# Prompt attention and convolution of a hybrid decoder step: other places in the interleaved order, compressed scores on column quarters, the convolution in five pieces

## The chip, the cores and the metric

The kernel runs on one core of one Trainium2 chip, in float32 throughout. The metric is the device time of one execution in microseconds (us). The engines are TensorE (PE, with PEld for its weight loads), VectorE (DVE), ScalarE (ACT), GpSimd (POOL) and SyncE (SP); SP issues most DMAs and POOL some. Each engine works through its own instructions in the order in which the program gives them to it.

## The reference, cut to what matters

One step of a hybrid decoder layer for 256 prompt rows and 8 sequences of 8 sample rows (320 columns together): a feed-forward half-step, one combined projection, a Mamba-2 mixer (convolution, chunked scan, gate), native sparse attention, a merge, and a second feed-forward half-step. The change touches the convolution and the prompt's attention:

```python
def causal_conv(xbc, conv_state, w, b):
    L = xbc.shape[1]
    xp = jnp.concatenate([conv_state.astype(xbc.dtype), xbc], axis=1)
    y = b + sum(xp[:, k:k + L] * w[k] for k in range(D_CONV))
    return jax.nn.silu(y), xp[:, L:]
...
    s_c = jnp.einsum('bthgd,bnhd->bthgn', q, kc) + bias_qk(dist_c, bias_tab)
    p_c = masked_softmax(s_c, (dist_c >= 0)[None, :, None, None, :])
    o_c = jnp.einsum('bthgn,bnhd->bthgd', p_c, vc)
    # and the same over selected blocks and over a window of the raw keys
    return gates[..., 0:1] * o_c + gates[..., 1:2] * o_s + gates[..., 2:3] * o_w
```

`kc` and `vc` are compressed keys and values, one per 32 rows, so the 256 prompt rows have 8 of them.

## The kernel before, in words

All weight matrices stream once through the core. `dense` (L329 to L355) multiplies one 128x1024 weight tile with the 320 activation columns: the tile comes by DMA, ACT makes its high part (L317, 1 us), DVE its low part (L326, 1.2 us), and PE runs 24 matmuls (8 steps k, three matmuls each, L345 to L347) into a PSUM bank `pd`. I call this a unit. Units follow each other through the whole program and keep PE busy.

Everything else is written as Python generators and put between the matmuls of the units when the program is built. After each k of a unit `dense` calls `S.tick()`. A tick moves a deferred function half a unit of `defer` nearer (`S.defer(2, f)` runs `f` four ticks later, and a unit has eight ticks), and adds half of `RATE[i]` to a credit; for each whole credit one step of a generator is emitted, up to its next `yield`. So RATE 1.5 puts six steps into a unit. Two chains of generators take turns; `pace(i)` sets the rate when a chain comes to a new part. Part 3 is prompt attention, part 4 the scan (`ssd`), part 5 the attention of the samples (`sample_attn`), part 6 `merge_prep`. The order on every engine is thus fixed when the program is built, and an instruction that has to wait holds up all that stands behind it on its engine.

The stretch in question has 24 units of the projection, whose outputs are the channels of the convolution. Behind each, `conv_unit` (L1218) works up its 320 columns:

- at once: POOL copies the old state (`scv`) into `pr`, ACT copies the unit's output into `pr` (L1222, L1223), POOL saves the new state (`ncv`, two small copies) and computes the first tap (`cvo`, L1229);
- four ticks later (`taps`): DVE adds three taps (L1233, three instructions), and directly behind them ACT takes the tanh (L1234);
- eight ticks later (`gate`): DVE forms the output `xbc` (L1237, L1240).

Beside it `prompt_attn` runs over 4 blocks `qc` of 64 queries and 8 pairs of heads `u`, 32 iterations `i`. For each block:

- `build(qc)`: POOL scales the queries into a tile of zeros, `qbp` (L1269, tile `blob`);
- `cmp_a(qc)`: PE multiplies the queries with the 2, 4, 6 or 8 compressed keys (L1276, tile `ps_pt`), then ten small instructions on DVE and ACT make a softmax of it;
- `cmp_b(qc, q)`, q = 0 and 1: PE transposes four heads' weights (L1298), ACT copies them out (L1299).

For each iteration: `scores` (PE L1305 into a bank `sc`, DVE bias and minimum L1311, ACT exponentials L1314), `norm` (DVE reciprocal L1322, POOL scaling L1325), `transposes` (PE L1337 into a bank `pt`, ACT copy L1338) and `values` (PE L1354 into the one bank `po`, which ACT empties at the end of a block, L1358). `scores` runs four iterations ahead of `values`. Behind `values` the block in work prepares the next: `build` at u = 1, `cmp_a` at u = 2, both `cmp_b` at u = 4.

The second chain first turns the values of the prompt into rows (`values_tok`, PE L1023 and L1029, ACT copies), then handles the samples' new keys (`new_keys`, PE L1041, L1055, L1068) and compressed keys (`cmp_sample`, PE L1127, L1182, L1200), which uses much DVE.

PSUM has eight banks: three `pd`, two `sc`, two `pt`, one `po`. A bank can be written again when its last reader is through.

## Time and profile before

| What | Value |
|---|---|
| Runs shown | 1339.16, 1340.64, 1348.0 us, median 1340.64 |
| Profiled execution | 1347.1 us, span from first to last instruction 1345.5 us |
| PE busy | 1277.8 us, 95% of the span |
| DVE busy | 877.8 us, 65% |
| ACT busy | 591.8 us, 44% |
| POOL busy | 371.0 us, 28% |
| Granted TensorE clock, mean | 0.973 |

PE does nearly all the time, so a place can be worth something only where PE stands still or where its clock is below full. A digit in the profile's slices hides the place of such a stand; the waits by engine, the sums by stretch and the timeline show it. A wait in these views is the idle time of an engine directly before an instruction, with the instruction elsewhere that ended it.

### The profile page before, as it was taken

The page shows a single profiled execution, that of the slowest core. Times are in us where ns is not written, and L with a number is a line of the kernel's source. Part 1 is how long each engine was busy: PE and PEld are TensorE (multiplying, and loading weights), DVE is VectorE, ACT ScalarE, POOL GpSimd, SP SyncE. Part 2 cuts the span into 40 slices and gives each one's busy share as a digit, 9 for nine tenths or more (in the row PEclk, how much of TensorE's full clock was granted, in tenths as well). Part 3 has the DMA queues.
Part 4 walks back from the last instruction along what each step waited for, and adds up shares of the span by engine and source line. Part 5 has one row for each costly group of instructions (what it writes and reads, how often), then busy time and mean ns, then how long its engine had stood idle before and what let it go on. Part 6 is the DMA issues. An engine that isn't in the chain of part 4 may idle for free. (4 is left out here: it accounts for less than half of the span.)

```text
span 1345.5 us, 28237 instructions
## 1 busy us (share of the span) xinstructions
PE 1277.8 (95%) x10609; PEld 1158.7 (86%) x10609; DVE 877.8 (65%) x1872; ACT 591.8 (44%) x1154; POOL 371.0 (28%) x624
## 2 busy tenths in 40 slices
PE   7999999999999998889999798998989999999998
PEld 7799999999989897777797576776758999999998
DVE  5267766755565767886568688778657766666543
ACT  4254444445435323455654243456554444333331
POOL 2123221322200225765435553344430010000000
PEclk8699999999989998999999999999999999999999
DMA  8256665766654435531157676899982544444553
GB/s 270 97 161 222 215 215 169 222 220 217 199 181 138 141 136 190 187 113 64 48 180 245 196 239 197 295 351 326 342 292 92 177 134 143 156 156 145 156 165 91
DMA packets 98467, 251.65 MB, mean 187 GB/s; under 512 B 14632, under 2 KB 41273, under 8 KB 96377
## 3 DMA queue, kind: packets, MB, share of 16 engines
q1 hardware_dynamic: 81370, 198.24, 44.9%
q0 software_dynamic: 16960, 51.61, 11.2%
q8 instruction: 84, 1.38, 0.4%
q14 instruction: 53, 0.43, 0.1%
HBM read 235.07 MB, written 23.10 MB: 192 GB/s over the span
## 5 line engine op out<-in xcount | busy, mean ns | idle before, releaser
L345 PE MATMUL ps_pd<-hh,wh 128*128 128x320 f32 x1320 | 444.5, 337 | 5.7 <-ACT hh L261 1.8
L326 DVE TENSOR_TENSOR wl<-wraw,wh 128x1024 fp32r<-128x1024 f32 (+1 forms) x245 | 305.4, 1248 | 183.2 <-ACT wh L317 176.2
L347 PE MATMUL ps_pd<-hh,wl 128*128 128x320 f32 x1320 | 416.4, 315 | 1.5 <-DVE wl L326 1.5
L346 PE MATMUL ps_pd<-hl,wh 128*128 128x320 f32 x1320 | 416.8, 316 | 0.6 <-DVE hl L454 0.3
L317 ACT CAST wh<-wraw 128x1024 fp32r<-128x1024 f32 (+1 forms) x245 | 252.2, 1032 | 139.7 <-PE ps_pd L346 102.2
L345 PEld LDWEIGHTS ps_pd<-hh,wh 128*128 128x128 f32 x1320 | 255.1, 193 | 30.1 <-issue 16.2
L346 PEld LDWEIGHTS ps_pd<-hl,wh 128*128 128x128 f32 x1320 | 255.7, 194 | 9.2 <-issue 4.8
L347 PEld LDWEIGHTS ps_pd<-hh,wl 128*128 128x128 f32 x1320 | 255.2, 193 | 2.2 <-DVE wl L326 2.2
L345 PE MATMUL ps_pd<-ah,wh 128*128 128x320 f32 x352 | 109.5, 311 | 0.0
L347 PE MATMUL ps_pd<-ah,wl 128*128 128x320 f32 x352 | 108.9, 309 | 0.0
L580 DVE TENSOR_TENSOR pgl<-pg,pgh 128x512 fp32r<-128x512 f32 x128 | 82.5, 685 | 30.0 <-ACT pgh L573 29.9
L346 PE MATMUL ps_pd<-al,wh 128*128 128x320 f32 x320 | 98.8, 309 | 0.0
L568 POOL DMA_DIRECT2D pg<-in_cache x136 | 74.2, 546 | 76.8 <-DVE pgl L580 30.8
L238 POOL TENSOR_SCALAR ah<-ff 128x320 fp32r<-128x320 f32 x44 | 20.0, 454 | 268.7 <-DVE ff L482 268.7
L477 ACT ACTIVATE sg<-sg 128x320 f32<-128x320 f32 x44 | 20.8, 472 | 134.2 <-DVE sg L476 134.1
L573 ACT CAST pgh<-pg 128x512 fp32r<-128x512 f32 x128 | 72.6, 616 | 9.1 <-PE ps_sc L702 8.8
L1419 POOL DMA_DIRECT2D KV<-in_cache x102 | 54.9, 539 | 76.7 <-PE ps_po L1506 43.2
L701 PE MATMUL ps_sc<-pgh,w1h 128*128 128x256 f32 x256 | 68.1, 287 | 0.8 <-ACT pgh L573 0.8
L702 PE MATMUL ps_sc<-pgh,w1l 128*128 128x256 f32 x256 | 68.1, 288 | 0.0
L345 PEld LDWEIGHTS ps_pd<-ah,wh 128*128 128x128 f32 x352 | 66.2, 188 | 0.5
L347 PEld LDWEIGHTS ps_pd<-ah,wl 128*128 128x128 f32 x352 | 66.1, 188 | 0.0
L346 PEld LDWEIGHTS ps_pd<-al,wh 128*128 128x128 f32 x320 | 60.2, 188 | 0.0
(474 smaller groups left out, 2219.6 us busy)
## 6 DMA issues: line engine op xcount, KB each, us to landing
wraw<-in_wproj SPq DMA_DIRECT2D x77, 512.0 KB
KV<-in_cache POOLq DMA_DIRECT2D x102, 256.0 KB, 5.6
wraw<-in_w1in SPq DMA_DIRECT2D x44, 512.0 KB
wraw<-in_w2in SPq DMA_DIRECT2D x44, 512.0 KB
pg<-in_cache POOLq DMA_DIRECT2D x136, 128.0 KB, 4.1
pg<-in_cache SPq DMA_DIRECT2D x120, 128.0 KB
wraw<-in_w1out SPq DMA_DIRECT2D x16, 512.0 KB
h<-in_ssm SPq DMA_DIRECT2D x32, 256.0 KB
```

The lines of the kernel that those rows point to most:

```text
L317: a.copy(h[:, :n], st["raw"][i][:, :n])
L326: v.tensor_tensor(l[:, :n], st["raw"].pop(i)[:, :n], st["hl"][i][0][:, :n], op=ALU.subtract)
L345: pe.matmul(out, wh[:, s], xh[:, kk, :], start=kk == 0, stop=False)
L346: pe.matmul(out, wh[:, s], xl[:, kk, :], start=False, stop=False)
L347: pe.matmul(out, wl[:, s], xh[:, kk, :], start=False, stop=kk == K - 1)
L477: a.activation(s, s, AF.Silu)
L568: e.dma_start(page(s, half)[:, i, :], I["cache"][ds(r, 1), :, 256 * c : 256 * c + 256].rearrange("o p f -> p (o f)"))
L573: a.copy(h[:, 8 * half : 8 * half + 8, :], page(s, half)[:, :, 64 * q : 64 * q + 64])
L580: v.tensor_tensor(l[:, 8 * half : 8 * half + 8, :], page(s, half)[:, :, 64 * q : 64 * q + 64], h[:, 8 * half : 8 * half + 8, :], op=ALU.su ...
L701: pe.matmul(ph, wh[:, j, :], h[:, :, j, :], start=q + j == 0, stop=False)
L702: pe.matmul(ph, wl[:, j, :], h[:, :, j, :], start=False, stop=False)
L1419: e.dma_start(t[:, j, :], I["cache"][ds(r, 1), :, 512:1024].rearrange("o p f -> p (o f)"))
```

## The change: what it does

Eight things, in the order of the diff:

1. `RATE[3]` (prompt attention) 1.5 to 1.55, `RATE[4]` (scan) 0.88 to 0.9.
2. The second transpose of `values_tok` uses a bank `sc` instead of `pt`.
3. `cmp_sample` has its four waiting steps spread between its reductions, and one step more before `mb`.
4. The convolution has five pieces: copies at once, then the first tap with the `ncv` copies (2 ticks), three taps (5 ticks), tanh (8 ticks), gate (11 ticks).
5. `cmp_a` runs each pair of heads as four matmuls of 32 query columns, each into its own quarter of the PSUM partitions, instead of one of 128 columns.
6. The first block: `build(0)`, five empty steps, then `scores(0)`, `cmp_a(0)`, `scores(1)` to `scores(3)`, `cmp_b(0, 0)`, `transposes(0)`, `cmp_b(0, 1)`, with steps between.
7. The next blocks: `build` at u = 0, `cmp_a` at u = 3.
8. The two `cmp_b` come at u = 5 and u = 6 instead of together at u = 4.

```diff
-RATE = (0.59, 1.2, 0.9, 1.5, 0.88, 0.57, 1.0)
+RATE = (0.59, 1.2, 0.9, 1.55, 0.9, 0.57, 1.0)
...
         for t in range(2):
-            pv = bank("pt")
+            pv = bank("sc" if t else "pt")
...
         for j in range(2):
             v.reduce_sum(rk[:, j, :], U[j], axis=AX.X)
+            yield
             v.reduce_sum(cs[:, j, :], U[j].rearrange("p i j -> p j i"), axis=AX.X)
-            yield from wait(2)
+            yield
...
         mb = pq.tile([128, 4, 2, 32], F32, name="mb")
+        yield
...
-        gcopy(ncv[:, i, 0:3], pr[:, 256:259])
-        gcopy(ncv[:, i, 3:27].rearrange("p (b k) -> p b k", b=NB), ps_[:, :, 8:11])
...
-        g.tensor_scalar(o, pr[:, 0:344], w(0), cwh[:, 96 + i : 97 + i], op0=ALU.mult, op1=ALU.add)
+
+        def first():
+            g.tensor_scalar(o, pr[:, 0:344], w(0), cwh[:, 96 + i : 97 + i], op0=ALU.mult, op1=ALU.add)
+            gcopy(ncv[:, i, 0:3], pr[:, 256:259])
+            gcopy(ncv[:, i, 3:27].rearrange("p (b k) -> p b k", b=NB), ps_[:, :, 8:11])
 
         def taps():
             for k in range(1, 4):
                 v.scalar_tensor_tensor(o, pr[:, k : k + 344], w(k), o, op0=ALU.mult, op1=ALU.add)
+
+        def tanh():
             a.activation(th, o, AF.Tanh)
...
-        S.defer(2, taps)
-        S.defer(4, gate)
+        S.defer(1, first)
+        S.defer(2.5, taps)
+        S.defer(4, tanh)
+        S.defer(5.5, gate)
...
             for u in range(8):
-                pe.matmul(pc[:, u, :nb], qbp[qc % 2][:, u, :], kTp[:, u // 4, :nb], start=True, stop=True)
+                for c in range(4):
+                    o = slice(32 * c, 32 * c + 32)
+                    pe.matmul(pc[o, u, :nb], qbp[qc % 2][:, u, o], kTp[:, u // 4, :nb], start=True, stop=True)
...
         build(0)
-        yield from wait(2)
+        yield from wait(5)
+        scores(0)
+        yield
         cmp_a(0)
-        yield from wait(4)
+        yield
+        scores(1)
+        yield
+        norm(0)
+        scores(2)
+        yield
+        norm(1)
+        scores(3)
+        yield
+        norm(2)
         cmp_b(0, 0)
+        yield
+        transposes(0)
+        yield
         cmp_b(0, 1)
-        for i in range(4):
-            scores(i)
-            yield
-            if i:
-                norm(i - 1)
-        transposes(0)
         yield
...
-                if u == 1:
+                if u == 0:
                     build(qc + 1)
-                elif u == 2:
+                elif u == 3:
                     cmp_a(qc + 1)
-                elif u == 4:
-                    cmp_b(qc + 1, 0)
-                    cmp_b(qc + 1, 1)
+                elif u in (5, 6):
+                    cmp_b(qc + 1, u - 5)
```

How the order changes is seen best on three engines. The first place is ACT at the end of block 0, where `po` is emptied (the copy `qn<-ps_po`). `cvt` is the tanh of the convolution, `pr` its input, `wh` the high part of a weight tile, `pT` and `blob` are transposes of `transposes` and `cmp_b`, `pS` the exponentials. Before:

```order
L1234 ACTIVATE cvt<-cvo 128x344
L1338 COPY pT<-ps_pt 128x256
L1314 ACTIVATE pS,pm<-pS,pm 128x128 x2
L1222 COPY pr_4873<-ps_pd 128x256
L1223 COPY pr_4873<-ps_pd 128x8x8
L317 CAST wh<-wraw 128x1024
L1358 COPY qn<-ps_po 128x8x64
```

With the change, on the same engine at the same place:

```order
L1240 ACTIVATE cvt<-cvo 128x344
L1309 COPY blob<-ps_pt 4x512
L1224 COPY pr_4873<-ps_pd 128x256
L1225 COPY pr_4873<-ps_pd 128x8x8
L317 CAST wh<-wraw 128x1024
L1348 COPY pT<-ps_pt 128x256
L1324 ACTIVATE pS,pm<-pS,pm 128x128 x2
L1368 COPY qn<-ps_po 128x8x64
L1240 ACTIVATE cvt<-cvo 128x344
```

The tanh that stood in the middle of a unit now stands at its end, directly before the copies of the next unit's output, three ticks behind its taps; what ACT does between two tanhs is the same as before in another order, and one copy of `cmp_b` comes into it. The emptying of `po` stands directly before a tanh in both.

The second place is POOL around `build(1)` (`blob<-qn`), with the scaling of `norm` (`pS<-pS,pm,gtp`) and the convolution's pieces. Before:

```order
L1308 MEMSET pS 128x2x64
L238 TENSOR_SCALAR pr_4873<-scv 128x8x3
L238 TENSOR_SCALAR ncv<-pr_4873 128x3
L238 TENSOR_SCALAR ncv<-pr_4873 128x24
L1229 TENSOR_SCALAR cvo<-pr_4873,cwh 128x344
L1269 TENSOR_SCALAR blob<-qn 64x8x64 x2
L1325 TENSOR_SCALAR pS<-pS,pm,gtp 128x64 x2
```

With the change, on POOL around the same `build(1)`:

```order
L1318 MEMSET pS 128x2x64
L238 TENSOR_SCALAR pr_4873<-scv 128x8x3
L1277 TENSOR_SCALAR blob<-qn 64x8x64 x2
L1231 TENSOR_SCALAR cvo<-pr_4873,cwh 128x344
L238 TENSOR_SCALAR ncv<-pr_4873 128x3
L238 TENSOR_SCALAR ncv<-pr_4873 128x24
L1335 TENSOR_SCALAR pS<-pS,pm,gtp 128x64 x2
```

`build(1)` now stands ahead of the pieces that read ACT's copy into `pr`, no longer behind them, and the first tap ahead of the two `ncv` copies.

The third place is PE at `cmp_a(1)`, directly behind an iteration's `values`. Before:

```order
L1354 MATMUL ps_po<-pT,vtp 64x64 x4
L1354 MATMUL ps_po<-blob,vcp 64x64 x2
L1276 MATMUL ps_pt<-kTp,blob 128x4 x8
L345 MATMUL ps_pd<-hh,wh 128x320
L346 MATMUL ps_pd<-hl,wh 128x320
```

With the change, on PE, one iteration later in the block:

```order
L1364 MATMUL ps_po<-pT,vtp 64x64 x4
L1364 MATMUL ps_po<-blob,vcp 64x64 x2
L1286 MATMUL ps_pt<-kTp,blob 32x4 x32
L345 MATMUL ps_pd<-hh,wh 128x320
L346 MATMUL ps_pd<-hl,wh 128x320
```

Eight matmuls of 128 query columns have become 32 of 32 columns (the profile counts each float32 matmul twice). Between `build(1)` and `cmp_a(1)` lie three iterations instead of one. For block 0, PE has 21 matmuls of units between L1041 of `new_keys` and the first use of the built queries before the change, and 45 with it, and that first use is `scores(0)` instead of `cmp_a(0)`.

In the scan, RATE 0.9 puts 3.6 steps into a unit instead of 3.52. Against the units, `ssd` begins one or two ticks earlier than before, and `sample_attn` begins and ends about three quarters of a unit earlier.

## Rows read from the trace of the kernel before

**Rows 1.** The page's span, and its busy time by engine (us, share of the span, instructions).

```profile
span 1345.5 us, 28237 instructions
...
PE 1277.8 (95%) x10609; PEld 1158.7 (86%) x10609; DVE 877.8 (65%) x1872; ACT 591.8 (44%) x1154; POOL 371.0 (28%) x624
```

**Rows 2.** Busy time by stretch, from the projection's units with `values_tok` to the end of the scan. Columns: the stretch and its length, then busy us of PE, PEld, DVE, ACT and POOL (with instructions), the granted clock as a share of full, the DMA share and GB/s.

```profile
494.00:515.00 21.00, 18.42 (x161) 17.08 (x161) 17.18 (x41) 6.65 (x15) 11.54 (x22) 1.00 0.42 143
515.00:530.00 15.00, 12.64 (x95) 12.31 (x92) 10.22 (x27) 3.80 (x10) 9.10 (x11) 0.77 0.34 125
530.00:545.00 15.00, 12.81 (x232) 11.69 (x232) 10.80 (x34) 8.65 (x29) 7.15 (x17) 1.00 0.65 250
545.00:580.00 35.00, 28.55 (x248) 25.28 (x248) 31.83 (x78) 16.31 (x54) 22.93 (x42) 0.95 0.56 207
580.00:600.00 20.00, 16.43 (x131) 14.81 (x130) 16.38 (x48) 8.82 (x30) 12.93 (x21) 0.91 0.23 76
600.00:625.00 25.00, 22.34 (x244) 18.52 (x243) 15.85 (x54) 14.39 (x44) 13.46 (x31) 1.00 0.17 57
625.00:690.00 65.00, 64.98 (x665) 54.87 (x663) 40.02 (x124) 37.93 (x104) 30.55 (x70) 1.00 0.26 82
690.00:865.00 175.00, 156.64 (x1101) 127.00 (x1107) 137.51 (x256) 73.47 (x161) 78.22 (x64) 1.00 0.71 227
```

**Rows 3.** What PE waited for from 495 to 690 us: the waiting line, what ended the wait, us in total, how often, the longest.

```profile
PE ps_pt L1276 <- POOL blob L1269: 4.4, 2, 2.4
PE ps_po L1354 <- ACT qn L1358: 3.6, 1, 3.6
PE ps_pt L1298 <- ACT pT L1338: 3.0, 1, 3.0
PE ps_pt L1023 <- DVE kTp L1115: 2.6, 1, 2.6
PE ps_pt L1337 <- POOL pS L1325: 1.7, 1, 1.7
PE ps_sc L1305 <- DVE pm L1311: 1.3, 1, 1.3
PE ps_pt L1337 <- ACT pT L1338: 1.0, 2, 0.6
PE ps_sc L1127 <- ACT otl L1071: 0.9, 1, 0.9
PE ps_pt L1337 <- ACT blob L1299: 0.7, 1, 0.7
```

**Rows 4.** PE's timeline around `values_tok` and the first three `cmp_a`. Columns: start and length in us, line and operation, in brackets the idle time before and what ended it.

```profile
509.90 0.66 PE L1023 MATMUL ps_pt<-con,vr 128*128 128x128 f32 x4 [2.58 <-DVE kTp L1115]
...
511.37 0.67 PE L1029 MATMUL ps_pt<-con,vr 128*64 128x128 f32 x8
...
517.02 0.31 PE L346 MATMUL ps_pd<-hl,wh 128*128 128x320 f32 x1
517.17 0.31 PE L347 MATMUL ps_pd<-hh,wl 128*128 128x320 f32 x1
...
521.60 2.98 PE L1276 MATMUL ps_pt<-kTp,blob 128*128 128x2 f32 x16 [2.36 <-POOL blob L1269]
...
526.40 0.47 PE L345 MATMUL ps_pd<-hh,wh 128*128 128x320 f32 x1
526.67 0.47 PE L346 MATMUL ps_pd<-hl,wh 128*128 128x320 f32 x1
...
557.36 1.95 PE L1276 MATMUL ps_pt<-kTp,blob 128*128 128x4 f32 x16 [2.03 <-POOL blob L1269]
...
603.10 1.95 PE L1276 MATMUL ps_pt<-kTp,blob 128*128 128x6 f32 x16
```

**Rows 5.** PE's timeline at the value product of `cmp_sample`, 32 matmuls of 32 columns each, in four quarters of the partitions, behind a matmul of a unit.

```profile
612.44 0.31 PE L347 MATMUL ps_pd<-hh,wl 128*128 128x320 f32 x1
612.68 1.10 PE L1200 MATMUL ps_sc<-kcv,cpT 128*32 128x64 f32 x64
```

**Rows 6.** What ACT and DVE waited for from 495 to 690 us, the longest of each; columns as in rows 3.

```profile
ACT cvt L1234 <- DVE cvo L1233: 39.0, 15, 5.7
ACT cvt L1234 <- DVE pm L1322: 22.8, 8, 4.0
...
DVE wl L326 <- ACT wh L317: 13.7, 10, 3.2
```

**Rows 7.** Timeline of DVE, ACT and POOL: `gate` and the copy that frees the bank of `values_tok`; `build(1)`; and the taps, the tanh and the emptying of `po` before block 1's first `values`.

```profile
509.00 0.43 DVE L1237 SCALAR_TENSOR_TENSOR xbc<-cvt,cvo 128x256 f32<-128x256 f32 x1 [0.61 <-ACT cvt L1234]
...
509.68 0.16 DVE L1115 COPY kTp<-ps_pt 128x16 f32<-128x16 f32 x1
...
555.14 2.16 POOL L1269 TENSOR_SCALAR blob<-qn 64x512 f32<-64x512 f32 x2
...
585.09 1.80 DVE L1233 SCALAR_TENSOR_TENSOR cvo<-pr,cwh,cvo 128x344 f32<-128x344 f32 x3
...
586.98 0.49 ACT L1234 ACTIVATE cvt<-cvo 128x344 f32<-128x344 f32 x1 [4.70 <-DVE cvo L1233]
...
589.94 0.59 ACT L1358 COPY qn<-ps_po 128x512 f32<-128x512 f32 x1
```

**Rows 8.** What PE waited for longest from 690 to 865 us, in the scan; columns as in rows 3.

```profile
PE ps_po L1807 <- DMA h<-in_ssm: 9.7, 6, 3.4
```

## The prediction

> **What bounds the kernel now.** I read the page's busy times first: PE is busy 1277.8 of 1345.5 us [rows 1], so the kernel ends when PE has done its work, and only PE's idle time and the time it spends at a lower clock can be won without taking work off it. Then the sums by stretch [rows 2]: idle time is the stretch's length less PE busy. From 494 to 625 us, where the convolution's units lie beside the second chain and the first half of prompt attention, it is 2.58 + 2.36 + 2.19 + 6.45 + 3.57 + 2.66 = 19.8 us. From 625 to 690 us it is 0.02: the second half of prompt attention has so much PE work that nothing is late. The scan from 690 to 865 us has 18.4 us. The change touches the first of these stretches, and the scan only by its rate.
>
> The granted clock is the second loss. It is 0.77 in 515 to 530 us, 0.95 in 545 to 580, 0.91 in 580 to 600, and full elsewhere [rows 2]. What it costs is (1 - clock) times the length: 3.5 + 1.8 + 1.8 = 7.0 us. In the timeline the step between a unit's matmuls is 0.15 us at full clock (517.02 to 517.17) and 0.27 us behind `cmp_a(0)` (526.40 to 526.67) [rows 4], which is the level of 1.2 GHz beside that of 2.4. So the stretch holds 19.8 + 7.0 = 26.8 us that are not work.
>
> Third, the waits of PE, which say what ended each idle time [rows 3]: 4.4 us for `build` on POOL, 9.2 us for copies on ACT (3.6 + 3.0 + 1.0 + 0.9 + 0.7), 2.6 us for one small copy on DVE, 3.0 us for POOL's scaling and the bank of `scores`. And last the waits of ACT itself: 39.0 + 22.8 = 61.8 us before the tanh of the convolution, always for DVE [rows 6]. ACT is not busy there, it stands in line: whatever stands behind the tanh (copies out of PSUM that free PE's banks, the high part of the next weight tile) waits for the taps. One instance is in the rows: DVE's taps run 585.09 to 586.89, the tanh starts at 586.98 after 4.70 us idle, and the emptying of `po` behind it at 589.94 [rows 7], and this is PE's longest wait, 3.6 us [rows 3].
>
> **The change part by part.** The sum is made against the profiled execution, 1347.1 us: its span of 1345.5 and 1.6 around it. It lies 6.5 us above the median of 1340.64, and I carry the difference over to the median.
>
> *The second transpose on `sc`.* PE waited 2.58 us for the copy of `kTp`, which holds the `pt` bank [rows 4]. With an `sc` bank it doesn't wait, but L1029 still needs that `pt` bank, and without the wait it would come at 511.37 - 2.58 = 508.8. The copy ended at 509.84, behind a `gate` that itself waited 0.61 us for a tanh [rows 7]; with the tanh three ticks ahead of its gate, that 0.61 goes, so it ends at 509.2. Some 0.5 us of the wait stays with its latency: saved 2.0 (bounds 1.5 and 2.6).
>
> *`build` earlier.* The two waits are 2.36 and 2.03 us [rows 4]. For block 0, 24 more matmuls of a unit lie between, 24 x 0.147 = 3.5 us, more than 2.36. For block 1, `build` stands on POOL ahead of the pieces that read ACT's copies, and three iterations lie between instead of one; it runs 2.16 us [rows 7]. Saved 4.4, all of it (bound from below 2.4, if the new `scores(0)` finds another operand late).
>
> *Compressed scores on quarters.* 16 PE instructions take 1.95 us at full clock [rows 4], 0.12 us each; four groups make 7.8. With the change there are 64. The nearest row is the product of `cmp_sample`: 64 instructions of 32 columns over four quarters in 1.10 us, 0.017 us each, and it starts 0.24 us behind the unit's matmul instead of 0.15 [rows 5]. It moves 64 columns, these 2 to 8. I take 1.1 us a group: saved 4 x 0.85 = 3.4. The other bound is that instructions that small don't overlap: 64 x 0.12 = 7.7 us, 23 us more in all. I take the row of the same form. The Trainium skill, TensorEngine Tiling (Array Packing), section "Instruction Overhead", says that a matmul with one moving column has the latency of one with 60 and that a factor shouldn't be taken from a dimension that is already small; by that, four times the instructions would cost 23 us. The row of 64 instructions in 1.10 us speaks against it, since they are in flight together.
>
> *The clock.* Two of the three falls follow a `build` wait and a `cmp_a` that keeps few columns moving, and the third the wait for `po` [rows 2, 3]. `cmp_a` alone doesn't do it: the third group, at 603.10, has no wait ahead of it, and the clock of that stretch is 1.00 [rows 2, 4]. I count 5.0 of 7.0 as gone (bounds 2 and 7). The Trainium skill, TensorE: Matmul & The Clock Gate, section "HAM oscillation", says that an engine which waits between bursts comes back at the low clock; by that all 7.0 go and the sum is 2 us better. Here the wait of 2.58 us at 509.90 left the clock at 1.00 [rows 2, 4], so a wait alone doesn't decide.
>
> *Five pieces, `cmp_b` in two.* The 9.2 us of waits for ACT go as far as they come from its standing behind a tanh. The taps take 1.8 us [rows 7], and the tanh now comes three ticks behind them: nine matmuls of a unit, 1.3 us, plus what an iteration puts between. Most of ACT's idling before the tanh should go, and with it some of DVE's 13.7 us of waiting for `wh` [rows 6]. `cmp_b` asks for one `pt` bank at a time. But ACT's exponentials still need DVE, and where DVE is late, ACT is. I take 6.0 (bounds 2 and 9.2), and 1.0 of the 3.0 for scaling and the bank of `scores`.
>
> *What DVE gives back.* From 545 to 600 us DVE is busy 31.83 + 16.38 = 48.2 of 55 us [rows 2], and the change takes no work off it. My savings there are 2.0 of `build`, 2.5 of clock, 0.9 of quarters and 6.5 of the rest, 11.9, which would ask for 48.2 us of DVE work in 43. It may run late into 600 to 625 us, where it is busy 15.85 of 25, but only as far as two `sc` banks allow. I give back 4.0. What is late next is then `scores`, for its bank.
>
> *New waits.* `new_keys`' transpose L1055 had `cmp_a(0)` ahead of it, and now follows L1041 by 24 matmuls, 3.5 us; L1068 now comes two scores after `cmp_a(0)`, whose ten small instructions stand on DVE ahead of its bank. 1.5 us for both (0 to 3).
>
> *The rates.* 1.55 with two more steps in the first block ends prompt attention a few ticks sooner: nothing. 0.9 makes the scan 2.3% denser. If the scan's own chain bounded all of 690 to 865 us, 2.3% of 175 us, 4.0 us, of unit work would lose its cover; if PE did, nothing. PE is idle 18.4 of 175 us and DVE busy 137.5 [rows 2]; the largest wait is 9.7 us for loads of the states [rows 8], which comes from few steps between load and use. I take 1.5 (0 to 4). The spreading of `cmp_sample`'s reductions is within the DVE term.
>
> Sum: 2.0 + 4.4 + 3.4 + 5.0 + 6.0 + 1.0 = 21.8 saved, 4.0 + 1.5 + 1.5 = 7.0 given back: 14.8 less, 1332.3 for such an execution, and 1340.64 - 14.8 = 1325.8 for the median. I say 1326.
>
> **The rivals.**
> *DVE takes the place of the waits.* DVE's queue is full from 545 to 600 us, so PE's idle time there comes back under another name (`scores` waiting for L1311, scaling waiting for DVE). Then only what lies before 545 us (2.0 + 2.4, 2.5 of clock) and half the quarters (1.7) remain, less 3.0 of new waits and rates: 5.6 saved, 1335. For it: 48.2 of 55 us. Against: some of DVE's time there is idling for `wh` that the tanh causes.
> *All of it goes.* 26.8 us and 3.4 of the quarters, nothing given back: 30 saved, 1311; with 1.5 of new waits and 4 for the scan, 1316. Against: the same 48.2 us.
> *Slower: the quarters don't overlap.* Place: the four `cmp_a`. At 0.12 us an instruction they cost 4 x 7.7 = 30.8 instead of 7.8 us: 23 more in place of 3.4 less, so 1325.8 + 26.4 = 1352. Without the quarters 11.4 us are saved, so it decides from 7.8 + 11.4 = 19.2 us for the four, 0.075 us an instruction. Against it are the 0.017 us of a form that differs only in its moving columns [rows 5]. For it speaks the rule of the Trainium skill named above, TensorEngine Tiling (Array Packing).
> *Slower: the scan.* Denser steps shift the loads of the states; 9.7 us of waits [rows 8] would have to more than double to eat the whole gain. At twice, 9.7 more and the 4.0 above: about 1338, no change.
>
> **How the numbers follow.** Forecast, 1320 to 1332: 0.55. DVE in place of the waits, 1332 to 1339: 0.20. All gone, 1311 to 1320: 0.10. The scan's loads, 1334 to 1345: 0.07. Quarters without overlap, 1345 to 1355: 0.04; other mechanisms that make it slower: 0.04. A range of 1314 to 1339 leaves out about 0.03 of the third case, half of the fourth and all of the last two, 0.15. A measurement can tell about 1% of this kernel from no change, 13.4 us: faster means below 1327.2, which holds 0.34 of the forecast's 0.55 and the third case: 0.44. Slower, above 1354: half the quarters' case and the 0.04, with 0.02 for what I overlook: 0.08. The rest, 0.48, is within 1%. The predicted time lies at the edge of the first two.
>
> **What would show it.** PE's waits for L1269's successor gone, and for L1023; clock 1.00 in 515 to 530 us; `cmp_a` as 64 instructions in 1.1 us; ACT's wait before the tanh down from 61.8 us to under 25; DVE's wait for `wh` below 13.7. PE idle in the stretch of 131 us down from 19.8 to about 8. Wrong would be: the same idle time with waits for DVE; quarters at over 0.05 us an instruction; the scan's 18.4 us grown by more than 5.

## The result, and the profile after

The changed kernel takes 1360.66 us (median of 4 runs, 1355.56 to 1368.83), the kernel before, on the same chip, 1342.81 us (4 runs, 1339.16 to 1348.0). The ratio is 1.0129, with a 95% interval of 1.0089 to 1.0168: slower by 1.3%, some 17 us. I had forecast 1326 and given "slower by over 1%" a chance of 0.08.

The profiled executions differ by less, 1355.6 against 1347.1 us, since the one of after was the shortest of its four and the one of before among the longer ones. So I compare stretch by stretch. ACT makes one high part `wh` for each weight tile, 245 in all, and I number these casts from 0: cast 92 stands at the beginning of the stretch that the change touches, 116 at the end of the convolution's units, 158 behind the samples' attention. ACT's timeline at casts 92, 116 and 158, of before and then of after:

```profile
496.75 1.06 ACT L317 CAST wh<-wraw 128x1024 fp32r<-128x1024 f32 x1
...
692.03 1.04 ACT L317 CAST wh<-wraw 128x1024 fp32r<-128x1024 f32 x1
...
1030.76 1.03 ACT L317 CAST wh<-wraw 128x1024 fp32r<-128x1024 f32 x1
```

```profile
488.26 1.06 ACT L317 CAST wh<-wraw 128x1024 fp32r<-128x1024 f32 x1
...
686.10 1.04 ACT L317 CAST wh<-wraw 128x1024 fp32r<-128x1024 f32 x1
...
1038.08 1.05 ACT L317 CAST wh<-wraw 128x1024 fp32r<-128x1024 f32 x1 [0.91 <-PE ps_pd L346]
```

Up to cast 92 both run the same program, and yet they lie 8.5 us apart. From 92 to 116 (the **first stretch**) before takes 195.28 us and after 197.84: 2.6 more, where I had forecast 16 less. From 116 to 158 (**scan and samples**) it is 338.73 against 351.98: 13.2 more, where I had forecast 1.5. From there to the end of the span it is 1.1 us more.

The page of after, busy times:

```profile
PE 1268.7 (94%) x10801; PEld 1148.2 (85%) x10801; DVE 874.1 (65%) x1872; ACT 591.4 (44%) x1154; POOL 370.4 (27%) x624
```

PE is busy for 9.1 us less than in [rows 1] and stands still for longer. The sums by stretch, at the places of [rows 2] shifted by 8 us:

```profile
486.00:507.00 21.00, 19.77 (x192) 18.62 (x191) 15.36 (x38) 6.62 (x15) 11.11 (x22) 1.00 0.40 132
507.00:522.00 15.00, 10.51 (x131) 9.81 (x129) 10.65 (x25) 4.04 (x11) 10.12 (x12) 1.00 0.60 213
522.00:537.00 15.00, 8.96 (x190) 8.02 (x191) 10.80 (x38) 7.13 (x27) 5.61 (x15) 0.66 0.55 204
537.00:572.00 35.00, 28.00 (x299) 24.47 (x297) 29.98 (x72) 14.78 (x48) 20.51 (x36) 0.95 0.52 198
572.00:592.00 20.00, 17.16 (x132) 14.58 (x133) 13.62 (x43) 10.94 (x36) 12.36 (x24) 0.91 0.16 54
592.00:617.00 25.00, 21.92 (x290) 18.36 (x290) 17.38 (x60) 13.02 (x41) 13.30 (x31) 0.93 0.20 65
...
682.00:857.00 175.00, 152.44 (x1016) 118.51 (x1015) 126.01 (x229) 68.31 (x152) 79.79 (x67) 0.96 0.65 203
```

Over the same 131 us PE is idle 1.23 + 4.49 + 6.04 + 7.00 + 2.84 + 3.08 = 24.7 us, where it was 19.8, and the clock costs 5.1 + 1.8 + 1.8 + 1.8 = 10.4, where it was 7.0. In the scan (the last row) PE is idle 22.6 us against 18.4, and the clock, which was full there in before, costs 0.04 x 175 = 7.0. What PE waits for (487 to 682 us), against [rows 3]:

```profile
PE ps_sc L1068 <- DVE pm L1332: 6.0, 1, 6.0
PE ps_pt L1347 <- ACT pT L1348: 5.0, 2, 4.8
...
PE ps_sc L1055 <- ACT ts L1050: 2.3, 1, 2.3
PE ps_sc L1315 <- DVE pm L1321: 2.2, 1, 2.2
```

The waits for `build` are gone. In their place stand waits for banks `sc` that DVE has yet to read. The timeline shows the largest (PE, then the DVE rows that it waits for):

```profile
516.36 0.71 PE L1286 MATMUL ps_pt<-kTp,blob 128*32 128x2 f32 x64
518.44 0.38 PE L1315 MATMUL ps_sc<-knp,blob 128*128 128x128 f32 x2
521.92 0.46 PE L1315 MATMUL ps_sc<-knp,blob 128*128 128x128 f32 x2 [2.23 <-DVE pm L1321]
529.30 0.33 PE L1068 MATMUL ps_sc<-vst,blob 64*32 64x64 f32 x4 [6.04 <-DVE pm L1332]
```

```profile
518.19 3.31 DVE L1237 SCALAR_TENSOR_TENSOR cvo<-pr,cwh,cvo 128x344 f32<-128x344 f32 x3
...
525.07 0.16 DVE L1291 TENSOR_TENSOR psc<-ps_pt,pb 128x16 f32<-128x16 f32 x1
...
527.07 1.79 DVE L1237 SCALAR_TENSOR_TENSOR cvo<-pr,cwh,cvo 128x344 f32<-128x344 f32 x3
528.78 0.22 DVE L1321 CUSTOM_DVE_ANT_0 pS<-ps_sc,pb 128x64 f32<-128x64 f32 x1
```

`scores(1)` is written at 518.44 and read at 528.78, because `cmp_a(0)`'s ten small instructions and the taps of a unit stand ahead of its reading; L1068 needs its bank. The first compressed scores themselves are fast: 64 instructions in 0.71 us, against 2.98 at the low clock in [rows 4].

What ACT and DVE wait for, against [rows 6] and this row of before:

```profile
ACT pS L1314 <- DVE pm L1311: 10.6, 14, 1.9
```

```profile
ACT pS L1324 <- DVE pm L1321: 38.6, 20, 7.3
ACT cvt L1240 <- DVE cvo L1237: 23.8, 8, 6.2
...
ACT cvt L1240 <- DVE kTp L1115: 4.0, 1, 4.0
...
ACT cvt L1240 <- DVE pm L1332: 2.9, 1, 2.9
...
DVE wl L326 <- ACT wh L317: 26.1, 14, 3.1
```

ACT's wait before the tanh fell from 61.8 to 30.7 us, but its wait before the exponentials rose from 10.6 to 38.6, and DVE now waits 26.1 us for `wh` instead of 13.7. Last, the waits of PE in scan and samples (682 to 857, then 857 to 1038 us, the last beside its row of before):

```profile
PE ps_po L1824 <- DMA h<-in_ssm: 8.4, 6, 3.7
PE ps_pt L410 <- DVE grs L256: 6.4, 1, 6.4
```

```profile
PE ps_po L1506 <- ACT R L1512: 4.5, 4, 1.8
...
PE ps_po L1523 <- ACT R L1529: 12.1, 6, 4.8
```

The loads of the states cost 8.4 us, less than the 9.7 of [rows 8]. New is L410, a group norm, which waits for DVE. Where does that come from? SP and POOL in before, around the store of the prompt's last state (`out_ssmP`) and the first load of the samples' cache (`KV`), which takes over that state's memory and so has to wait for the store (the profile names the store in after; in before it names a DVE instruction):

```profile
837.00 6.78 SPq L1711 DMA_DIRECT2D out_ssmS<-h  x4
843.82 0.42 SPq L1711 DMA_DIRECT2D out_ssmP<-St  x1
...
839.84 2.07 POOL L1809 TENSOR_TENSOR h<-h,cdb 128x512 f32<-128x512 f32 x2 [6.11 <-issue]
847.28 1.16 POOL L1419 DMA_DIRECT2D KV<-in_cache  x2 [5.38 <-DVE grs L256]
848.46 2.49 POOL L1809 TENSOR_TENSOR h<-h,cdb 128x512 f32<-128x512 f32 x2
```

And in after, with the DVE instructions around it:

```profile
834.05 5.59 SPq L1728 DMA_DIRECT2D out_ssmS<-h  x4
841.04 0.34 SPq L308 DMA_DIRECT2D wraw<-in_wproj  x1
841.43 0.42 SPq L1728 DMA_DIRECT2D out_ssmP<-St  x1
...
833.44 2.08 POOL L1826 TENSOR_TENSOR h<-h,cdb 128x512 f32<-128x512 f32 x2 [2.95 <-DMA h<-in_ssm]
847.57 1.16 POOL L1436 DMA_DIRECT2D KV<-in_cache  x2 [12.06 <-DMA out_ssmP<-St]
848.75 2.08 POOL L1826 TENSOR_TENSOR h<-h,cdb 128x512 f32<-128x512 f32 x2
...
838.60 1.29 DVE L1831 TENSOR_TENSOR h<-h,ps_sc 128x512 f32<-128x512 f32 x2 [5.07 <-PE ps_sc L1830]
...
849.85 0.69 DVE L1831 TENSOR_TENSOR h<-h,ps_sc 128x512 f32<-128x512 f32 x1 [8.44 <-POOL h L1826]
```

A weight load has slipped ahead of the store on SP. From the end of POOL's product to the issue of the store it is 843.82 - 841.91 = 1.9 us in before and 841.43 - 835.52 = 5.9 in after, and from there to the `KV` load 3.5 and 6.1. Of the 5.9 the weight load's own part is 841.43 - 839.64 = 1.8: the last `out_ssmS` ahead of it is not issued earlier, because the addition on DVE that it stores waited 5.07 us for PE. So POOL stands at that load for 12.06 us instead of 5.38; behind it stand the next products of the states, behind those DVE's additions, and behind those the small instructions of the norm.

Later, `R` (L1523) has one buffer, which ACT and DVE must have read first. Its longest wait, with what ACT, DVE and PE do there:

```profile
933.18 2.97 ACT L261 CAST yh<-xbc 128x320 fp32r<-128x320 f32 x8
933.66 3.30 DVE L264 TENSOR_TENSOR yl<-xbc,yh 128x320 fp32r<-128x320 f32 x8 [1.03 <-ACT yh L261]
...
940.77 1.08 PE L1523 MATMUL ps_po<-KV,sT 128*32 128x64 f32 x32 [4.80 <-ACT R L1529]
```

Eight casts and eight differences for the next weights, which stand at a fixed unit, fall into the middle of a sample's work here.

### The profile page after: what moved, and what is told of

Its sections match the earlier page's. It is cut to its first block, busy times and chain, and to the rows that moved or that the text cites. A ratio compares the mean times of both kernels' runs of the same rounds, so it can differ in the third digit from the quotient of the medians.

```text
span 1353.9 us, 28627 instructions
## 1 busy us (share of the span) xinstructions
PE 1268.7 (94%) x10801; PEld 1148.2 (85%) x10801; DVE 874.1 (65%) x1872; ACT 591.4 (44%) x1154; POOL 370.4 (27%) x624
## 5 line engine op out<-in xcount | busy, mean ns | idle before, releaser
L345 PEld LDWEIGHTS ps_pd<-hh,wh 128*128 128x128 f32 x1320 | 252.9, 192 | 29.4 <-issue 14.7
L568 POOL DMA_DIRECT2D pg<-in_cache x136 | 74.2, 546 | 76.5 <-DVE pgl L580 30.7
```

Of the source, the lines that this page charges most:

```text
L345: pe.matmul(out, wh[:, s], xh[:, kk, :], start=kk == 0, stop=False)
L568: e.dma_start(page(s, half)[:, i, :], I["cache"][ds(r, 1), :, 256 * c : 256 * c + 256].rearrange("o p f -> p (o f)"))
```

## The experiments

Each is given as ratio to before, and by the two stretches of its trace (us more than before, worked out from the casts as above). "Place" says where the samples' first scores stand among the steps of the units, eight steps to a unit, in the order of PE's instructions.

| Kernel | Ratio, 95% interval | First stretch | Scan, samples | Place |
|---|---|---|---|---|
| after | 1.0129, 1.0089 to 1.0168 | +2.6 | +13.2 | 113.75 |
| e1_rates_back | 1.0065, 1.0034 to 1.0096 | +0.3 | +7.6 | 114.875 |
| e2_scan_rate_alone | 1.0147, 1.0102 to 1.0192 | -0.3 | +17.8 | 113.75 |
| e3_conv_old | 1.0110, 1.0075 to 1.0145 | -2.8 | +14.6 | 113.75 |
| e4_conv_alone | 1.0019, 0.9989 to 1.0050 | +5.0 | +3.4 | 114.375 |
| e5_order_old | 0.9997, 0.9973 to 1.0021 | +1.9 | -1.4 | 113.375 |
| e6_quarters_alone | 0.9958, 0.9934 to 0.9982 | -3.2 | -1.1 | 114.375 |
| e7_vtok_spread_alone | 1.0039, 1.0009 to 1.0068 | -3.0 | +14.7 | 114.5 |
| e8_order_alone | 1.0038, 1.0006 to 1.0070 | +3.7 | +12.4 | 114.75 |
| e9_cache_behind | 1.0087, 1.0053 to 1.0122 | +3.7 | +9.7 | 113.75 |
| e10_after_later | 1.0047, 1.0021 to 1.0073 | +2.6 | +3.8 | 114.375 |
| e11_before_later | 1.0061, 1.0033 to 1.0089 | -0.9 | +10.6 | 114.5 |
| e12_quarters_bank | 0.9991, 0.9963 to 1.0018 | -3.3 | +0.7 | 114.375 |
| e13_quarters_cache | 0.9957, 0.9928 to 0.9986 | -3.3 | -2.0 | 114.375 |
| e14_first_block | 1.0087, 1.0056 to 1.0117 | +7.0 | +8.1 | 114.75 |
| e15_later_blocks | 0.9984, 0.9959 to 1.0010 | +0.7 | +5.2 | 114.375 |
| e16_tanh_at_taps | 1.0054, 1.0025 to 1.0083 | +7.1 | -1.4 | 114.375 |

Before has place 114.375, so the change moves these scores 0.625 of a unit earlier. Two traces are longer than their kernel's median, e8 by 11 us and e15 by 15, so of these two the ratio weighs more. Each trace is a single execution. In the first stretch, where e2, e11 and before are the same program, their lengths differ by up to 0.9 us, but what they are made of differs by more: PE is idle 16.5, 15.6 and 19.8 us, and the clock costs 10.2, 12.0 and 6.8.

**Which part loses.** Two kernels with one part undone (e1 and e3, their diffs against after) and two with one part alone (e2 and e4, against before).

```diff
-RATE = (0.59, 1.2, 0.9, 1.55, 0.9, 0.57, 1.0)
+RATE = (0.59, 1.2, 0.9, 1.5, 0.88, 0.57, 1.0)
```

> The kernel after with the two rates of before (1.5 for prompt attention, 0.88 for the scan). Three theories of the 18 us lost (medians 1342.8 before, 1360.7 after). S, the later stages: the rate of the scan and what it shifts behind it (loads of the states, POOL's loads of the samples' cache, PE's waits for R in the sample stage) cost most of it; then this kernel gets back at least 9 us, to about +2 to +9 us against before. P, the order of the prompt's first block: PE's waits of 2.3, 2.2 and 6.0 us at 511 to 530 us for banks and copies that stand behind cmp_a(0) and the scores on DVE; then at most 4 us come back, +14 or more. C, the five pieces of the convolution: at most 4 us come back as well.

Measured +8.7 us (0.65% of 1343): 8.6 of the 17 come back, 2.3 of them in the first stretch. For S, at the upper end.

```diff
-RATE = (0.59, 1.2, 0.9, 1.5, 0.88, 0.57, 1.0)
+RATE = (0.59, 1.2, 0.9, 1.5, 0.9, 0.57, 1.0)
```

> The kernel before with the scan's rate at 0.9 and nothing else. S: +8 to +13 us against before, since the rate alone shifts the scan and the sample stage. P and C: within 3 us of before.

Measured +20 us, more than the whole change and more than S had allowed, nearly all of it in scan and samples. P and C can't give that.

```diff
-        S.defer(1, first)
-        S.defer(2.5, taps)
-        S.defer(4, tanh)
-        S.defer(5.5, gate)
+        S.defer(2, taps)
+        S.defer(4, gate)
```

> The kernel after with the convolution in the pieces of before (tap and copies at once, taps with tanh after four ticks, gate after eight). C: at least 9 us come back, +9 us or less against before. S and P: it stays at +14 or more, or gets worse, as ACT stands behind the tanh again (the prediction's 6 us: +20 to +24).

Measured +14.8 us: not C's. But the first stretch is 2.8 us shorter than before and 5.3 shorter than after, the reverse of my term.

```diff
-        S.defer(2, taps)
-        S.defer(4, gate)
+        S.defer(1, first)
+        S.defer(2.5, taps)
+        S.defer(4, tanh)
+        S.defer(5.5, gate)
```

> The kernel before with the convolution in five pieces and nothing else. C: +8 us or more against before. S and P: -6 to 0 us, by the prediction's own term for ACT no longer standing behind the tanh.

Measured +2.6 us, with no clear sign; its first stretch is 5.0 us longer. None of the theories had this.

**The other parts.** The order undone (e5, against after), then quarters, bank with spread steps, and order alone (against before).

```diff
-                elif u in (5, 6):
-                    cmp_b(qc + 1, u - 5)
+                elif u == 4:
+                    cmp_b(qc + 1, 0)
+                    cmp_b(qc + 1, 1)
...
```

> The kernel after with the order of prompt attention of before (first block, places of build, cmp_a and cmp_b); quarters, five pieces, rates and the bank of the values stay as in after. P (the new first block puts PE's products of the samples' new keys behind banks that wait for DVE): at least 9 us come back, +9 us or less against before. S (the rates) and C (five pieces): at most 4 us come back, +14 or more.

Measured -0.4 us: the whole loss is gone, as P had it. But the gain is not where P looked: the first stretch is 0.7 us better than after's, scan and samples 14.6. And the rate is still 0.9. So S in its plain form (the rate costs) fell here, too.

```diff
-                pe.matmul(pc[:, u, :nb], qbp[qc % 2][:, u, :], kTp[:, u // 4, :nb], start=True, stop=True)
+                for c in range(4):
+                    o = slice(32 * c, 32 * c + 32)
+                    pe.matmul(pc[o, u, :nb], qbp[qc % 2][:, u, o], kTp[:, u // 4, :nb], start=True, stop=True)
```

> The kernel before with the compressed scores on four column quarters and nothing else. The trace of after shows 64 instructions in 0.7 us where before 16 took 1.95 us (2.98 at the low clock); if that lands on the total, -4 to -6 us against before. If the time that the matmuls took covered work of DVE and ACT which PE has to wait for anyway, -1 to +1.

Measured -5.6 us, faster than before.

```diff
-            pv = bank("pt")
+            pv = bank("sc" if t else "pt")
...
-            yield from wait(2)
+            yield
...
+        yield
         v.memset(mb, 0.0)
```

> The kernel before with the second transpose of the values in a bank sc and the spread steps of the samples' compressed scores, nothing else. By the prediction's term -2 us against before; if one more step and another bank shift what follows, anything from -5 to +8, which would say that the total answers to the shift more than to the wait.

Measured +5.2 us. The first stretch is 3.0 us shorter, scan and samples 14.7 longer. Nothing in the edit belongs to the scan; but it moves it by one step of a unit.

```diff
-        yield from wait(2)
+        yield from wait(5)
+        scores(0)
+        yield
         cmp_a(0)
...
```

> The kernel before with the new order of prompt attention and nothing else. P: +8 us or more against before. S and C: -8 to 0 us, by the prediction's terms for the two waits for build and the clock behind them.

Measured +5.1 us: between the theories, again, by a long trace, with the larger part in scan and samples.

So a new theory, Z: what costs is the place of scan and samples against the units, whatever moved it. Four kernels for that, three of them without any other edit.

**The place, and the queue.** e9 and e10 are against after, e11 and e12 against before.

```diff
             s4.close()
+            for _ in range(1):
+                yield IDLE
             yield from early_kv()
```

> The kernel after with the first loads of the samples' cache (KV) one step later beside the scan, so that on POOL they stand behind the last two products of the scan's states instead of ahead of them; nothing else moves against the units. Theory Q, the queue: in after POOL stands 12.1 us at the first KV load until the store of the prompt's state (out_ssmP) is through, because on SP a weight load stands ahead of that store, and the state products, DVE's additions and PE's group norm (6.4 us) wait behind it. By Q 5 to 9 us of the 17 come back: +8 to +12 us against before. Rival: the wait only moves, to the loads or to the sample stage; then +14 or more.

Measured +11.7 us: 5.6 of the 17 are back, as Q had it, but the intervals of e9 and after overlap, so the trace has to show it. POOL in this kernel, products first:

```profile
837.64 1.06 POOL L1828 TENSOR_TENSOR h<-h,cdb 128x512 f32<-128x512 f32 x1 [1.56 <-PE ps_po L1826]
846.27 1.16 POOL L1436 DMA_DIRECT2D KV<-in_cache  x2 [7.57 <-DVE zth L2009]
```

The wait at L410 is gone from the trace, and casts 128 to 137, where after takes 82.88 us against 73.41 of before, take 75.82. So 7.1 us are back at that place; from cast 137 to 158, though, e9 is 3.4 longer than after, so that scan and samples as a whole gain 3.5. The rival, that the wait only moves to the samples, has about half of it.

```diff
-chain(pace(3), prompt_attn(), pace(4), ssd(), ...
+chain(pace(3), prompt_attn(), wait(4), pace(4), ssd(), ...
```

> The kernel after with four empty steps between prompt attention and the scan, so that the scan and the samples' attention stand at the same ticks of the units as in before (the samples' first scores at 114.375 of the units that the list counts, instead of 113.75), at the rate 0.9 of after. Theory Z, the place: the place of the scan against the units costs 13 us and the rate as such nothing; then +1 to +6 us against before, which is what the first stretch loses. Rival R, the rate: the denser steps cost it; then +11 or more.

Measured +6.3 us, just above Z's range and clear of after's interval. Four empty steps take back 11 us, with the rate still at 0.9: for Z, against R. PE's idle time in scan and samples falls from 38.0 to 25.7 us (before: 28.2).

```diff
-chain(pace(3), prompt_attn(), pace(4), ssd(), ...
+chain(pace(3), prompt_attn(), wait(1), pace(4), ssd(), ...
```

> The kernel before with one empty step between prompt attention and the scan and nothing else: scan and samples' attention come one to two ticks later, and on SP the weight load comes to stand ahead of the store of the prompt's state. Theory Z: +5 to +13 us against before, as in the run with the bank and the spread steps, whose shift is the same. Rival: that run lost its time by the spread steps themselves; then within 3 us of before.

Measured +8.2 us. One empty step in the kernel before costs 0.6%, all in scan and samples: for Z. POOL stands 10.76 us at the `KV` load here, too, and this wait of PE behind it is new:

```profile
PE ps_pt L1835 <- DVE ys L1823: 6.7, 1, 6.7
```

```diff
-            pv = bank("pt")
+            pv = bank("sc" if t else "pt")
...
+                for c in range(4):
...
```

> The kernel before with the compressed scores on quarters and the values' second transpose in a bank sc, neither of which moves a step: scan and samples stand where they stood. If the terms of the first stretch add up, -5 to -9 us against before (quarters alone gave 5.6, the bank 2 to 3 more). If the bank's 2 to 3 us are taken by the next wait, -4 to -6.

Measured -1.2 us, interval from -5.0 to +2.4, outside both ranges. Its first stretch is that of the quarters alone (-3.3 and -3.2): the bank gives 0.1 there. PE's wait at L1023 (2.7 us in e6) is gone, but 1.3 are left at L1029, and the wait for the first `build` is 1.5 longer. Why the median lies above that of e6 its trace doesn't show (the sum of its stretches is -2.6), and the two intervals overlap.

**What the first stretch loses, and a better version.**

> The kernel before with the compressed scores on quarters and the first loads of the samples' cache one step later beside the scan (POOL then has the last products of the states first). Nothing else moves. If POOL's wait of 5.4 us at that load costs before something as well, -6 to -10 us against before, a version that beats both. If in before other work covers it (no wait of PE there names the group norm or POOL), it stays at the quarters' -3 to -6.

(The edits of e6 and e9, on before.) Measured -5.8 us, faster than both kernels, and no better than the quarters alone: nothing shows that POOL's 5.38 us in before cost anything.

```diff
-        yield from wait(2)
+        yield from wait(5)
+        scores(0)
...
```

> The kernel before with the new first block of prompt attention alone (build, five empty steps, scores ahead of cmp_a). It ends two steps later, so the scan moves too; read from the trace, over the first stretch (24 units and the end of the attention): +3 to +5 us if PE's waits for banks and copies behind cmp_a(0) on DVE make the order's loss (3.7 us in the run with the whole order), 0 or less if the places in the later blocks make it.

(The first block of the change's diff, without the later places.) Measured +11.7 us; first stretch +7.0, more than expected. PE is idle 4.8 + 2.2 us at L1068 (6.0 in after; the profile names DVE for the 4.8 alone), and waits 7.7 for the second block's `build`, which has its old place here.

```diff
-                if u == 1:
+                if u == 0:
                     build(qc + 1)
-                elif u == 2:
+                elif u == 3:
                     cmp_a(qc + 1)
...
```

> The kernel before with the new places of build (u = 0), cmp_a (u = 3) and cmp_b (u = 5 and 6) alone. No step moves, so scan and samples stand where they stood. By the prediction's term for block 1's wait for build (2.0 us) and the clock behind it: -2 to -4 us in the first stretch and against before. If what is won there is a wait for DVE in another place: within 1 us.

Measured -2.2 us, interval from -5.5 to +1.3: no change that can be told.

```diff
             for k in range(1, 4):
                 v.scalar_tensor_tensor(o, pr[:, k : k + 344], w(k), o, op0=ALU.mult, op1=ALU.add)
+            a.activation(th, o, AF.Tanh)
...
-        S.defer(4, tanh)
```

> The kernel before with the convolution's first tap and taps deferred as in the five pieces, and the tanh directly behind the taps as before. The run with five pieces alone lost 5.0 us in the first stretch of its trace. If the tanh's place (directly ahead of the next unit's copies and high part) makes that, -1 to +1 us in the stretch here; if the later taps make it, +4 to +6.

(Against e4; the gate stays at 11 ticks, too.) Measured +7.3 us, first stretch +7.1: the later first tap, taps and gate lose, not the tanh's own place, which by these two traces won 2 of it (e4 has +5.0). Most of it is clock, right behind `values_tok` (one window; then PE's timeline):

```profile
508.00:524.00 16.00, 14.76 (x113) 13.82 (x114) 9.09 (x22) 5.91 (x15) 9.51 (x14) 0.57 0.54 190
```

```profile
508.46 0.66 PE L1023 MATMUL ps_pt<-con,vr 128*128 128x128 f32 x4 [2.54 <-DVE kTp L1115]
...
510.77 1.13 PE L1029 MATMUL ps_pt<-con,vr 128*64 128x128 f32 x8 [0.77 <-ACT vtp L1024]
...
515.32 3.59 PE L1041 MATMUL ps_sc<-ksm,qbs 128*64 128x8 f32 x64
```

At 0.57 of full speed these 16 us hold 6.9 us of lost clock, and e4 has the same at the same place. Over the first stretch the clock costs 15.4 us here and 18.8 in e4, against 6.8 to 12.0 in the three traces of the unchanged program; PE's idle time, 20.6 and 15.9, lies about where it lay there (15.6 to 19.8). The new wait of 0.77 us is for ACT's copy of the values, which stands behind a tanh whose taps now come later.

## Why the prediction was wrong, point by point

The forecast of 14.8 us less was missed in two places: scan and samples lost 13.2 where I had 1.5 (11.7 off), and the first stretch lost 2.6 where I had 16.3 less (18.9 off, of which the five pieces are 11.3).

**Quarters: right.** I took 3.4 us; alone they give 5.6 (2.4 to 8.9), 3.2 of it in the first stretch. In after a group of 64 instructions takes 0.71 or 0.72 us, 0.011 each, below the 0.017 that I read from [rows 5]. The factor of four was taken from the 128 query columns, which are not a small dimension, so what I had set against the split as a rival did not bear on it.

**The rates: the step that failed most.** I allowed 1.5 us, 4 at most, as if a denser scan could only lack cover. What the rate does as well is to move every instruction of scan and samples against the units, and +13.2 of the change's loss lies there. e2 shows that the scan's rate alone costs 20 us, e11 that one empty step, with no change of rate, costs 8, e10 that putting the old place back at the new rate returns 11. All seven kernels at place 114.375 lie between -2.0 and +5.2 there (+3.8 without e15's long trace), all at 113.75 and from 114.5 to 114.875 between +7.6 and +17.8; e5, at 113.375, has -1.4. PE's idle time in that stretch sorts by the place as well: 23.5 to 28.2 us in these seven and in before, 29.6 to 38.6 in all the others. So neither earlier nor denser is bad as such, and I know no rule for a good place. The rates were not the only part that moved it: first block, spread steps and rates all did, and their effects don't add (+20 by rate, +8 by a step, +17 together).

**The mechanism.** My rival "the scan" had the right region, with a chance of 0.07 and the wrong cause: the loads of the states didn't grow (8.4 against 9.7). Two waits come with the place. The first is POOL's standing at the `KV` load, with the products behind it; e9 shows what it is worth in after, 7.1 us where it stands and 3.5 in scan and samples together. The weight load ahead of the store is read, not tested: it is there in after, e3, e7, e8, e9, e11 and e14, where POOL stands 7.6 us (e9) to 12.1, and in none of the others, where it stands 3.4 to 8.0. But e1 and e2 lose without it. The second is only read: PE's waits for `R` are 12.1 to 12.7 us in all four kernels at 113.75 and 2.8 to 7.5 in all others; the longest in after, 4.8 us, comes behind the eight casts and differences. No run took that alone away. Why the other places cost what they do, and the rest of the 13 us, stays open.

**`build` earlier: the wait went, the time didn't.** Its rows are gone, as predicted, but "new waits" was sized 1.5 and measured 2.3 + 2.2 + 6.0 = 10.5. I had named the cause, the ten small instructions ahead of L1068's bank, and not counted that a unit's taps come between them and the reading. e14 puts the order's loss on the first block, and the later places alone give nothing measurable (e15); but undoing the whole order in the change gives back only 0.7 in the first stretch (e5).

**Five pieces: the sign was wrong.** I took 6.0 saved; the trace shows 5.0 lost alone (e4) and 5.3 lost within the change (after against e3). ACT does wait less before the tanh, but DVE is what is late: ACT's waits for DVE before tanh and exponentials were 61.8 + 10.6 = 72.4 us and are 30.7 + 38.6 = 69.3. My rival "DVE takes the place of the waits" had this mechanism, with 1335 us, and I gave it 0.20. That says why nothing was saved. What was lost in e4 and e16 is mostly clock. Within the change it isn't: the clock costs 10.2 in the first stretch of after and of e3, PE is idle 2.4 longer in after, and the rest of the 5.3 stays open.

**The bank.** 2.0 predicted, 0.1 found (e12 against e6): the wait moved to what follows. In e7, with the spread steps and without the quarters, the first stretch is 3.0 shorter; which of the two edits does that no run shows.

**The clock: wrong in its sign, and looked at in one stretch alone.** 5.0 predicted as gained; in the first stretch it costs 3.4 more. I had counted on the waits going. In scan and samples, for which the sum had no term of the clock, (1 - clock) times the length is 15.4 us in after against 5.1 in before, beside 38.0 against 28.2 of idle PE. e10 takes the idle time back and none of this (15.4); in e11's trace it is the other way round, 1.9 us more of idle time and 11.9 more of clock. The granted clock of every run says the same of the whole span: on average it costs 43.2 us in after (4 runs) and 34.5 in before (23 runs beside e1 to e4). Over 120 runs of before the time rises by 0.6 us for each us of clock lost; an estimate from these is that some 5 of the 17 us are clock, with four runs of after behind it. What makes it fall more often no run isolates.

The parts alone, -3.0 (bank and spread steps), -3.2 (quarters), +3.7 (order) and +5.0 (five pieces), make +2.5 in the first stretch, and after has +2.6. That is luck: the order's +3.7 comes from a long trace and is 0.7 within the change (e5), beside the quarters the bank gives 0.1 (e12), and the rates, which this sum leaves out, are 2.3 (e1).

## What to carry to other kernels

Where a counter puts work between the steps of other work, an edit that adds, drops or speeds up one step moves everything behind it, and the cost there can be ten times what the edit was for (20 us for the rate in e2, where I had allowed 1.5). Test such an edit with the place of what follows held (empty steps do it), and try that place as a size of its own; judge the edit's own gain by its own stretch of the trace, with PE's idle time and the lost clock apart, since one trace is one execution. A wait for an engine that is behind goes from one waiter to the next when the waiters are put in another order: count the late engine's waits over all lines together, and take work off it.

## What the runs showed of the hardware

All kernels are one and the same program up to cast 92, and yet the traces reach it at 485.0 us (e9) at the earliest and at 496.8 in before. The time goes with the granted clock up to there: 0.979 in e9 and in after (488.3), 0.982 in e4 (485.4), 0.952 in before. Over all 18 traces it is later by 0.7 us for each us of clock lost.

A wait of 2.58 us ahead of `values_tok`'s second transpose left the clock at 1.00 in before [rows 2, 4]; 2.54 us at the same place, with 0.77 more a little later, was followed by 16 us at 0.57 in e16 and in e4. But e11 and e2 are the same program as before up to there, with the same wait of 2.58 us, and in the 10 us from that wait on the clock was 0.83 in e11 and 1.00 in e2. So neither the wait nor the 0.77 is shown to decide.

Three taps on DVE take 1.8 us in most cases; the three at 518.19 in after took 3.31, beside a POOL product of 2.16 us, and so did the three at 527.98 in before, beside the same product. The Trainium skill, SBUF — State Buffer, section "Who interferes with whom", says that a DVE instruction with two inputs in SBUF contends with a GpSimd instruction that reads SBUF; both instances agree with it, and no run here takes the POOL instruction away. POOL in after, at that place:

```profile
518.35 2.16 POOL L1060 TENSOR_TENSOR blob<-tpT,con 128x1024 f32<-128x1024 f32 x1 [1.83 <-DVE tpT L1057]
```
